# Rotary's swapped halves in one VectorE step, and the product with 1/rms of queries and keys on POOL, in a two-layer encoder trunk

## The chip, the cores and the metric

The kernel runs on one core of one Trainium2 chip. The core has TensorE (PE in the profile, with its weight loads as PEld), VectorE (DVE), ScalarE (ACT), GpSimd (POOL) and a queue of SyncE (SP) that issues most DMAs. The metric is the time of one execution on the device in microseconds (us), lower is better; a kernel's time is the median of its runs. Before the change it is 1128.28 us, the median of three runs from 1127.73 to 1128.44.

## The reference

A trunk of two transformer layers over 512 tokens of width 1024, all in float32. Each layer has a token mixer with 12 query heads and 3 key/value heads of width 64, four more heads that attend to a memory of 256 tokens, an output projection, and a SwiGLU feed-forward of width 2816, each with RMS norms around it. Layer 0 (mixer A) attends in a band of 128 tokens to either side, with a sink logit per head, and rotates only the first 16 of 64 dimensions. Layer 1 (mixer B) attends globally, normalises every query and key head by its own RMS, and rotates all 64 dimensions by row and column of a grid:

```python
def apply_rotary(x, cos, sin):
    half = x.shape[-1] // 2
    x1, x2 = xf[..., :half], xf[..., half:]
    return jnp.concatenate([x1 * c - x2 * s, x2 * c + x1 * s], axis=-1)
...
def mixer_b(q, k, v, qk_g, cos_r, sin_r, cos_c, sin_c):
    q = axial_rope(rms_norm(q, qk_g[0]), cos_r, sin_r, cos_c, sin_c)
    k = axial_rope(rms_norm(k, qk_g[1]), cos_r, sin_r, cos_c, sin_c)
```

So a head x becomes x * cos plus its swapped halves times a signed sine, and in layer 1 the whole is multiplied by 1/rms(x). The factor 1/rms is one number per token and head, so it may be multiplied in before or after the rotation.

## The kernel before

**Numbers in two parts.** Float32 products are made of three TensorE products of a high and a low part (type fp32r). `split` (lines 252 to 262) makes them: ScalarE rounds the high part (L258), VectorE subtracts it to get the low part (L262). Flags in the table `PACE` send some of either to POOL (L256, L260). Weights, hidden rows, queries, keys, and probabilities all pass through such a split.

**The mixer.** Tokens are in four tiles of 128 rows (t = 0 to 3). Keys and values come first (`kv_pieces`), then queries in groups of four heads (`q_pieces`, c = 0 to 2, and c = 3 for the memory heads). One tile of a query group runs like this: TensorE multiplies the hidden rows with the weights, 24 matmuls of 256 columns (L248 to L250); ScalarE copies the result out as `qx` (L488 in layer 1, L490 in layer 0); `rope` rotates it in place; ScalarE and VectorE split it into `q2` (L258, L262); TensorE transposes it (L502), and ScalarE copies the transpose into `qT` (L503). Keys do the same in 192 columns as `kx`, with a copy of the high part on POOL (L380) and transposes at L387 and L392.

**Rotary.** `rope_a` (layer 0, L400 to L403) works on 16 of 64 elements of each head: two VectorE products write the swapped halves times the sine into `rt`, one multiplies `x` with the cosine in place, one adds. `rope_b` (layer 1) has on ScalarE the squares (L411), on VectorE their sum per head (L412), on POOL 1/rms in two steps, a multiply-add and a power (`rstd`, L276 and L277, tile `r`), and on VectorE the two products of the halves (L419), the product with the cosine (L420), the sum (L421) and the product with 1/rms (L422). There are 16 such tiles in each layer: four of keys, twelve of queries. L258 of `q` or `k` waits for L422.

**Attention.** `score` makes a head's scores for one tile of queries (L526, L527), VectorE takes the row minimum of the negated scores (L537; with mask and sink in layer 0, L532), ScalarE the exponential with its sum (L538). After the fourth tile `normalise` inverts the sums on VectorE (L574, tile `rd`) and POOL scales the four tiles `p` (L577). `turn` transposes `p` on TensorE (L587) into one of two PSUM buffers `tp`, which a split empties into `th` (ScalarE) and `tl` (VectorE); `value` multiplies them with V (L601, L602), and ScalarE and VectorE add the two halves of the result into `tok` (L609, L610).

**What sets the order.** TensorE's order is written out by hand: `mixer` puts every piece into a list with a due time, taken from `PACE`, and issues the pieces in the order of these times. Queries of group c + 1 are made while the heads of group c attend. On the other engines a planner orders the instructions when the kernel is built: it simulates the engines with costs of its own and lets each take, of what is ready, the instruction that stands first in the program. In the trace VectorE's steps of one rotation are thus mixed with row minima and splits. On the chip each engine then runs its list strictly in order and waits on semaphores.

Of the kernel before, what the change touches and what calls it, by code (L numbers as in the profile page):

```python
# [13 lines left out]
OP = mybir.AluOpType  # L14
AX = mybir.AxisListType

P = 128
# [8 lines left out]
HD = 64  # L26
# [153 lines left out]
class Trunk:  # L180
# [212 lines left out]
        nc.vector.tensor_copy(kb[:, :, c], tp[:, :n])  # L393


    def rope_a(self, x, t, n):
        v = self.nc.vector
        tmp = self.core.tile([P, 4, 16], F32, tag="rt", name="rt", bufs=2)
        cs, sn = self.ropet[:, 0, t], self.ropet[:, 1, t]
        v.tensor_mul(tmp[:, :n, 0:8], x[:, :n, 8:16], sn[:, None, 0:8].to_broadcast([P, n, 8]))  # L400
        v.tensor_mul(tmp[:, :n, 8:16], x[:, :n, 0:8], sn[:, None, 8:16].to_broadcast([P, n, 8]))
        v.tensor_mul(x[:, :n, 0:16], x[:, :n, 0:16], cs[:, None, :].to_broadcast([P, n, 16]))
        v.tensor_add(x[:, :n, 0:16], x[:, :n, 0:16], tmp[:, :n])  # L403

    def rope_b(self, x, t, n, z):

        nc = self.nc
        v = nc.vector
        sq = self.core.tile([P, 4, HD], F32, tag="rt", name="sq", bufs=2)
        ss = self.small.tile([P, 4], F32, tag="ss4", name="ss4", bufs=2)  # L410
        nc.scalar.activation(sq[:, :n], x[:, :n], AF.Square)  # L411
        v.tensor_reduce(ss[:, :n], sq[:, :n], axis=AX.X, op=OP.add)  # L412
        r = self.small.tile([P, 4], F32, tag="r4", name="r4", bufs=3)
        self.rstd(r[:, :n], ss[:, :n], HD)
        tmp = self.core.tile([P, 4, HD], F32, tag="rt", name="rt", bufs=2)
        gc, gs = self.gt[:, z, 0, t], self.gt[:, z, 1, t]
        for h in range(2):
            o, i = slice(32 * h, 32 * h + 32), slice(32 - 32 * h, 64 - 32 * h)
            v.tensor_mul(tmp[:, :n, o], x[:, :n, i], gs[:, None, o].to_broadcast([P, n, 32]))  # L419
        v.tensor_mul(x[:, :n], x[:, :n], gc[:, None, :].to_broadcast([P, n, HD]))  # L420
        v.tensor_add(x[:, :n], x[:, :n], tmp[:, :n])  # L421
        v.tensor_mul(x[:, :n], x[:, :n], r[:, :n, None].to_broadcast([P, n, HD]))  # L422

    def rope(self, l, x, t, n, z):
        (self.rope_b(x, t, n, z) if l else self.rope_a(x, t, n))
# [794 lines left out]
```

## Time and profile before

| | |
|---|---|
| median of three runs | 1128.28 us (1127.73 to 1128.44) |
| profiled execution, its own time | 1127.18 us |
| its span, first to last instruction | 1125.4 us |
| granted TensorE clock | 0.999 |
| share of the span that engines are busy | PE 98%, PEld 89%, VectorE 75%, ScalarE 59%, POOL 19% |

The slices of 1/40 of the span (28 us each) show where each engine is busy, in tenths:

```profile
PE   9999999999999999999999999999999999999997
DVE  5788885999448757875888998757996378669854
ACT  6678984765435624563567888756664255345631
POOL 5693331102000000000445643312000000000001
```

The attention of layer 0 lies in the first six slices, that of layer 1 in slices 20 to 26; there POOL is in use, while the two feed-forwards use it hardly at all. A row of a timeline has the start (us from the first instruction), the time taken, engine, line, operation, what it writes and reads, how many instructions were merged, and in brackets the idle time before it with what ended it. Rows of waits give the waiting instruction, the one that ended the wait, the sum in us, how many, and the longest.

### The profile page before, as it was taken

The page shows a single profiled execution, that of the slowest core. Times are in us where ns is not written, and L with a number is a line of the kernel's source. Part 1 is how long each engine was busy: PE and PEld are TensorE (multiplying, and loading weights), DVE is VectorE, ACT ScalarE, POOL GpSimd, SP SyncE. Part 2 cuts the span into 40 slices and gives each one's busy share as a digit, 9 for nine tenths or more (in the row PEclk, how much of TensorE's full clock was granted, in tenths as well). Part 3 has the DMA queues.
Part 4 walks back from the last instruction along what each step waited for, and adds up shares of the span by engine and source line. Part 5 has one row for each costly group of instructions (what it writes and reads, how often), then busy time and mean ns, then how long its engine had stood idle before and what let it go on. Part 6 is the DMA issues. An engine that isn't in the chain of part 4 may idle for free.

```text
span 1125.4 us, 19486 instructions
## 1 busy us (share of the span) xinstructions
PE 1098.2 (98%) x7463; PEld 1004.6 (89%) x7463; DVE 841.8 (75%) x1431; ACT 658.8 (59%) x1347; POOL 214.6 (19%) x356
## 2 busy tenths in 40 slices
PE   9999999999999999999999999999999999999997
PEld 7899988899889989998897888878999899899985
DVE  5788885999448757875888998757996378669854
ACT  6678984765435624563567888756664255345631
POOL 5693331102000000000445643312000000000001
PEclk9999999999999999999999999999999999999999
DMA  6521016443413322325542100145135123413243
GB/s 236 197 85 39 20 57 220 155 132 124 151 38 113 132 94 76 113 90 192 187 150 76 39 20 18 40 149 188 38 113 168 58 75 113 150 61 99 88 166 112
DMA packets 34220, 123.02 MB, mean 109 GB/s; under 512 B 3920, under 2 KB 4304, under 8 KB 34000
## 3 DMA queue, kind: packets, MB, share of 16 engines
q1 hardware_dynamic: 33984, 121.66, 32.5%
q8 instruction: 58, 0.95, 0.3%
q14 instruction: 34, 0.28, 0.1%
q10 hardware_dynamic: 144, 0.14, 0.0%
HBM read 111.29 MB, written 10.49 MB: 108 GB/s over the span
## 4 chain that ended last, share of the span: by engine, by line
PE 66%; DVE 7%; ACT 4%; POOL 2%; issue 2%; POOLq 0%; DVEq 0%; ACTq 0%
PE ps L954 12%; PE ps L955 12%; PE ps L956 12%; PE ps L249 9%; PE ps L248 9%; PE ps L250 9%; PE tp L587 1%; DVE wlo L262 1%; POOL r L277 1%; PE o L602 1%; ACT whi L258 1%; DVE nm L537 1%; PE o L601 1%; DVE tl L262 1%; ACT p L538 1%
## 5 line engine op out<-in xcount | busy, mean ns | idle before, releaser
L258 ACT ACTIVATE whi<-raw 128x512 fp32r<-128x512 f32 (+2 forms) x190 | 157.1, 840 | 184.5 <-PE ps L956 94.7
L262 DVE TENSOR_TENSOR wlo<-raw,whi 128x512 fp32r<-128x512 f32 (+2 forms) x178 | 171.7, 974 | 69.9 <-ACT whi L258 69.1
L954 PE MATMUL ps<-sf,whi 128*128 128x256 f32 x640 | 179.9, 281 | 0.2
L955 PE MATMUL ps<-sf,wlo 128*128 128x256 f32 x640 | 179.8, 281 | 0.0
L956 PE MATMUL ps<-sf,whi 128*128 128x256 f32 x640 | 179.7, 281 | 0.0
L248 PE MATMUL ps<-whi,f 128*128 128x512 f32 x352 | 137.2, 390 | 0.0
L249 PE MATMUL ps<-wlo,f 128*128 128x512 f32 x352 | 137.1, 389 | 0.0
L250 PE MATMUL ps<-whi,f 128*128 128x512 f32 x352 | 137.0, 389 | 0.0
L956 PE MATMUL ps<-a,whi 128*128 128x256 f32 x480 | 134.4, 280 | 0.0
L954 PE MATMUL ps<-a,whi 128*128 128x256 f32 x480 | 134.3, 280 | 0.0
L955 PE MATMUL ps<-a,wlo 128*128 128x256 f32 x480 | 133.8, 279 | 0.0
L954 PEld LDWEIGHTS ps<-sf,whi 128*128 128x128 f32 x640 | 121.1, 189 | 1.1 <-ACT p L960 0.6
L955 PEld LDWEIGHTS ps<-sf,wlo 128*128 128x128 f32 x640 | 121.4, 190 | 0.5
L956 PEld LDWEIGHTS ps<-sf,whi 128*128 128x128 f32 x640 | 121.4, 190 | 0.0
L286 POOL TENSOR_SCALAR e<-sso 128x1 f32<-128x1 f32 x8 | 3.4, 422 | 566.1 <-ACT junk L281 566.0
L248 PE MATMUL ps<-whi,hT 128*128 128x256 f32 (+1 forms) x320 | 98.8, 309 | 0.0
L577 POOL TENSOR_SCALAR p<-p,rd 128x256 f32<-128x256 f32 (+2 forms) x128 | 79.1, 637 | 99.2 <-DVE rd L574 53.1
L249 PE MATMUL ps<-wlo,hT 128*128 128x256 f32 (+1 forms) x320 | 94.0, 294 | 2.1 <-DVE wlo L262 1.9
L250 PE MATMUL ps<-whi,hT 128*128 128x256 f32 (+1 forms) x320 | 93.7, 293 | 0.0
L955 PEld LDWEIGHTS ps<-a,wlo 128*128 128x128 f32 x480 | 90.5, 188 | 0.2
L954 PEld LDWEIGHTS ps<-a,whi 128*128 128x128 f32 x480 | 90.4, 188 | 0.2
L956 PEld LDWEIGHTS ps<-a,whi 128*128 128x128 f32 x480 | 90.1, 188 | 0.0
(201 smaller groups left out, 2750.7 us busy)
## 6 DMA issues: line engine op xcount, KB each, us to landing
raw<-in_wgu_dram SPq DMA_DIRECT2D x48, 512.0 KB, 4.4
raw<-in_wd_dram SPq DMA_DIRECT2D x44, 512.0 KB, 4.2
rb<-in_wgu_dram SPq DMA_DIRECT2D x40, 512.0 KB, 3.6
raw<-in_wq_dram SPq DMA_DIRECT2D x16, 512.0 KB, 4.5
raw<-in_wo_dram SPq DMA_DIRECT2D x16, 512.0 KB, 3.6
xt<-x SPq DMA_DIRECT2D x12, 512.0 KB, 4.6
raw<-in_wm_dram SPq DMA_DIRECT2D x8, 512.0 KB, 4.1
x<-y SPq DMA_DIRECT2D x8, 512.0 KB, 2.9
```

The lines of the kernel that those rows point to most:

```text
L248: mm(out, lh, rh, start=first, stop=False)
L249: mm(out, lh, rl, start=False, stop=False)
L250: mm(out, ll, rh, start=False, stop=last)
L258: nc.scalar.activation(hi, src, AF.Copy)
L262: nc.vector.tensor_sub(lo, src, hi.bitcast(F32))
L277: g.tensor_tensor(r, r, self.mhalf[:, :r.shape[1]], op=OP.pow)
L537: nc.vector.tensor_reduce(nm[:, i:i + 1], s[:, :n], axis=AX.X, op=OP.min)
L538: nc.scalar.activation(p[:, :n], src[:, :n], AF.Exp, bias=nm[:, i:i + 1], scale=-1.0, accum_out=den[:, i:i + 1])
L577: self.pooled = nc.gpsimd.tensor_scalar(hd["p"][z][:, :n], hd["p"][z][:, :n], rd[:, z:z + 1], 1.0, op0=OP.mult, op1=OP.mult)
L954: mm(out, wh[:, s], rh, start=start and k == 0, stop=False, skip_group_check=True)
L955: mm(out, wl[:, s], rh, start=False, stop=False, skip_group_check=True)
L956: mm(out, wh[:, s], rl, start=False, stop=k == 3, skip_group_check=True)
```

## The change

Both rotations now write the swapped halves in one VectorE step. `halves` views the last dimension as two halves; the input is read with the order of the halves reversed, a negative stride of one half, 8 elements in layer 0 and 32 in layer 1. That is one VectorE instruction less per tile, in all 32 tiles. In layer 1 the last product, with 1/rms, goes to POOL, which makes 1/rms in the two steps before it: 16 instructions leave VectorE's queue and enter POOL's, and the split of the tile on ScalarE and VectorE now waits for POOL.

```diff
+    def halves(self, x):
+        return x.rearrange("p n (h d) -> p n h d", h=2)
+
     def rope_a(self, x, t, n):
...
-        v.tensor_mul(tmp[:, :n, 0:8], x[:, :n, 8:16], sn[:, None, 0:8].to_broadcast([P, n, 8]))
-        v.tensor_mul(tmp[:, :n, 8:16], x[:, :n, 0:8], sn[:, None, 8:16].to_broadcast([P, n, 8]))
+        v.tensor_mul(self.halves(tmp[:, :n]), self.halves(x[:, :n, 0:16])[:, :, ::-1],
+                     self.halves(sn[:, None, :].to_broadcast([P, n, 16])))
...
     def rope_b(self, x, t, n, z):
...
-        for h in range(2):
-            o, i = slice(32 * h, 32 * h + 32), slice(32 - 32 * h, 64 - 32 * h)
-            v.tensor_mul(tmp[:, :n, o], x[:, :n, i], gs[:, None, o].to_broadcast([P, n, 32]))
+        v.tensor_mul(self.halves(tmp[:, :n]), self.halves(x[:, :n])[:, :, ::-1],
+                     self.halves(gs[:, None, :].to_broadcast([P, n, HD])))
         v.tensor_mul(x[:, :n], x[:, :n], gc[:, None, :].to_broadcast([P, n, HD]))
         v.tensor_add(x[:, :n], x[:, :n], tmp[:, :n])
-        v.tensor_mul(x[:, :n], x[:, :n], r[:, :n, None].to_broadcast([P, n, HD]))
+        nc.gpsimd.tensor_tensor(x[:, :n], x[:, :n], r[:, :n, None].to_broadcast([P, n, HD]), op=OP.mult)
```

## The prediction

> **What bounds the kernel now.** I read the page first, then the stretches that hold the rotary steps, then the waits of TensorE in those stretches.
>
> ```profile
> span 1125.4 us, 19486 instructions
> PE 1098.2 (98%) x7463; PEld 1004.6 (89%) x7463; DVE 841.8 (75%) x1431; ACT 658.8 (59%) x1347; POOL 214.6 (19%) x356
> ```
>
> TensorE is busy for 98% of the span. All idle time of TensorE together is 1125.4 - 1098.2 = 27.2 us, and no change to VectorE or POOL can win more than its part of that. The change touches two stretches: the mixer of layer 0 (here 15 to 116 us) and that of layer 1 (here its queries, from 584 us). The columns of the next view are the stretch, its length, and the busy time of PE, PEld, DVE, ACT and POOL.
>
> ```profile
> 15.00:116.00 101.00, 97.43 (x726) 92.04 (x725) 81.64 (x227) 76.23 (x205) 64.55 (x106) 1.00 0.31 108
> 584.00:605.00 21.00, 19.30 (x139) 17.39 (x138) 16.67 (x42) 12.43 (x30) 9.19 (x14) 1.00 0.32 100
> 605.00:672.00 67.00, 62.70 (x436) 54.80 (x435) 63.24 (x128) 56.52 (x133) 40.56 (x50) 1.00 0.08 25
> ```
>
> The last row matters most. There VectorE is busy for 63.24 of 67 us, more than TensorE, so two engines share the bound; POOL has 26 us free. What TensorE waits for, from 584 to 672 us:
>
> ```profile
> PE tp L587 <- DVE tl L262: 2.2, 3, 1.0
> PE ps L249 <- DVE wlo L262: 1.1, 1, 1.1
> PE o L601 <- DVE tok L610: 0.9, 1, 0.9
> PE tp L587 <- POOL p L577: 0.9, 2, 0.5
> PE tp L502 <- DVE q L262: 0.5, 1, 0.5
> ```
>
> and from 15 to 120 us:
>
> ```profile
> PE tp L315 <- DVE mT L262: 1.4, 1, 1.4
> PE tp L587 <- POOL p L577: 1.1, 2, 0.8
> PE tp L587 <- DVE tl L262: 0.3, 1, 0.3
> PE tp L587 <- DVE qx L402: 0.2, 1, 0.2
> ```
>
> So 5.6 us of waits in layer 1, of which 4.7 us end with VectorE, and in layer 0 some 1.9 us that end with it. These few microseconds are what can be won, and a wait on POOL already stands among them.
>
> **The change part by part.** The durations are minimum / median / maximum in ns.
>
> ```profile
> L400 DVE TENSOR_TENSOR rt<-qx,cst x12: 159/193/525, 42.5 to 110.1; 128x32 f32<-128x32 f32 x12
> L401 DVE TENSOR_TENSOR rt<-qx,cst x12: 183/186/1348, 42.6 to 110.1; 128x32 f32<-128x32 f32 x12
> L402 DVE TENSOR_TENSOR qx<-qx,cst x12: 214/226/580, 42.8 to 110.8; 128x64 f32<-128x64 f32 x12
> L419 DVE TENSOR_TENSOR rt<-qx,gt x24: 275/284/1385, 584.6 to 664.6; 128x128 f32<-128x128 f32 x24
> L420 DVE TENSOR_TENSOR qx<-qx,gt x12: 408/418/909, 585.3 to 665.5; 128x256 f32<-128x256 f32 x12
> L422 DVE TENSOR_TENSOR qx<-qx,r x12: 407/426/861, 587.1 to 667.4; 128x256 f32<-128x256 f32 x12
> L621 POOL TENSOR_TENSOR gt<-ru x2: 737/1228/1720, 274.2 to 274.9; 128x256 f32<-128x256 f32 x2
> ```
>
> One step for the two halves. Two operations of layer 1 (2 x 284 ns) become one over 256 elements, which L420 prices at 418: 150 ns less per tile, 2.4 us over 16 tiles if the narrower key tiles save as much. In layer 0 it is 193 + 186 - 226 = 153 ns, again about 2.4 us. No row shows a negative stride. Inside a half the elements still lie side by side, so I take the plain price; the bounds are that (0.41 us) and every element at half speed (2 x 418 = 0.84 us). [...]
>
> The product with 1/rms. L422 leaves VectorE: 12 x 0.426 us, and for the four key tiles at three quarters of the width as an estimate 4 x 0.32, together 6.4 us. POOL gets 16 products of two inputs. L621 is the same kind and size on POOL: 0.74 us for the first, 1.72 for the second. I take 0.74, the undisturbed one, and keep 1.72 as the upper bound. For 16 that is up to 11.8 us, and POOL has the room. VectorE sheds 2.4 + 6.4 = 8.8 us in layer 1. What that is worth depends on the place.
>
> First group of queries. A wait is removed here, and a chain made longer.
>
> ```profile
> 588.02 0.43 DVE L262 TENSOR_TENSOR q<-qx,q 128x256 fp32r<-128x256 f32 x1 [0.48 <-ACT q L258]
> 588.50 0.53 PE L502 MATMUL tp<-identr,q 128*128 128x128 f32 x4
> 592.42 0.51 PE L502 MATMUL tp<-identr,q 128*128 128x128 f32 x4 [0.48 <-DVE q L262]
> 593.94 0.43 DVE L421 TENSOR_TENSOR qx<-qx,rt 128x256 f32<-128x256 f32 x1
> 595.26 0.43 DVE L422 TENSOR_TENSOR qx<-qx,r 128x256 f32<-128x256 f32 x1 [0.90 <-POOL r L277]
> 595.61 1.28 DVE L262 TENSOR_TENSOR wlo<-raw,whi 128x512 fp32r<-128x512 f32 x2
> 596.34 0.39 PE L249 MATMUL ps<-wlo,hT 128*128 128x256 f32 x1 [1.13 <-DVE wlo L262]
> ```
>
> The transposes of the first two tiles start 0.05 us after, or wait for, the split that ends the rotary chain. A product of 0.74 in place of 0.43 puts 0.31 us on each: +0.62 us (0, if ScalarE evicts the next tile ahead of the waiting split, to 2 x 1.29 = 2.6 with the long product). Behind the waiting split stand on ScalarE the eviction of the next tile and the key copies. The third tile pays in the other direction: VectorE stood 0.90 us waiting for r, with the weight split that TensorE needed behind it. Without L422 that split follows L421 at 594.37 instead of 595.61, 1.24 us earlier, and the wait of 1.13 us goes: -1.13 us (0 to -1.13). Next late is nothing that the view shows.
>
> The first head's probabilities.
>
> ```profile
> 612.88 1.01 POOL L277 TENSOR_TENSOR r<-r,mhalf 128x4 f32<-128x4 f32 x1
> 613.88 3.24 POOL L577 TENSOR_SCALAR p<-p,rd 128x512 f32<-128x512 f32 x4
> 614.46 0.41 DVE L421 TENSOR_TENSOR qx<-qx,rt 128x256 f32<-128x256 f32 x1
> 615.39 0.41 DVE L422 TENSOR_TENSOR qx<-qx,r 128x256 f32<-128x256 f32 x1
> 617.18 0.33 PE L587 MATMUL tp<-cst,p 128*128 128x128 f32 x1 [0.44 <-POOL p L577]
> ```
>
> TensorE takes each of these p as POOL finishes it. The product becomes ready at 614.87, in the middle of the four, and stands earlier in the program, so I put it between them: +0.74 us (0 behind them; if POOL waits for it ahead of them, 614.87 - 613.88 + 0.74 = +1.7). For the next head the view has:
>
> ```profile
> 619.93 3.13 POOL L577 TENSOR_SCALAR p<-p,rd 128x512 f32<-128x512 f32 x4 [0.82 <-DVE rd L574]
> 625.21 0.60 PE L587 MATMUL tp<-cst,p 128*128 128x128 f32 x4
> ```
>
> Its four p end at 623.06 and its transposes start at 625.21, which covers one product; I take the same for the heads behind it.
>
> The crowded stretch. Four waits, 2.2 us for tl and 0.9 for tok, end with VectorE.
>
> ```profile
> 629.25 0.43 DVE L422 TENSOR_TENSOR qx<-qx,r 128x256 f32<-128x256 f32 x1 [0.31 <-POOL r L277]
> 629.60 0.68 DVE L262 TENSOR_TENSOR tl<-tp,th 128x512 fp32r<-128x512 f32 x1
> 637.56 2.87 POOL L577 TENSOR_SCALAR p<-p,rd 128x512 f32<-128x512 f32 x4
> 637.66 0.86 DVE L422 TENSOR_TENSOR qx<-qx,r 128x256 f32<-128x256 f32 x1
> ```
>
> Ahead of each stands an L422 that goes: with its wait 0.74 us in the first, 0.86 us in the second, about 0.41 in the calmest, and the merged step gives 0.15 more each. That covers the three tl waits and over half of the tok wait: 2.2 + 0.5 = 2.7. L422 took 0.86 instead of 0.41 with POOL scaling p beside it; POOL's own products will stretch other two-input steps in the same way, so I give one such lengthening back: 2.7 - 0.4, -2.3 us (0 to -3.1).
>
> Layer 0. The wait for mT and the two short ones stand behind keys' and queries' rotary steps: 0.15 us each, -0.45 us (0 to -1.9).
>
> **Sum:** 0.62 - 1.13 + 0.74 - 2.3 - 0.45 = -2.5 us. The profiled execution took 1127.18 us around its span of 1125.4, 1.10 us under the median of 1128.28; the sum gives 1124.7 for it, and on the scale of the median 1125.8 us.
>
> **The rivals.**
>
> [...] A two-input product on POOL and two-input steps on VectorE lengthen each other: L421's kind of step takes 0.41 to 0.86 us, L621 0.74 to 1.72. If each of 16 products costs VectorE the 0.43 us that L422's worst row shows, 6.9 of the 8.8 us return, the crowded stretch wins 0.5 instead of 2.3, by the fifth of the relief that is left, and the rest (-0.2) remains: 1128.28 - 0.7 = 1127.6. For it speaks that POOL is busy 40.56 of 67 us there; against it that the steps reading PSUM (tl, row maxima) run at their usual length beside it. A stride that halves the rate ends in the same place: 16 x (0.84 - 0.57) = 4.3 us come back. [...]
>
> The queue makes it slower. POOL runs in order. If the products stand behind the four p, the one at 614.87 starts at 617.12 and ends at 617.86, 2.1 us later than L422 ended (615.80). ScalarE keeps its order, so its split of q holds the exponentials and probability copies behind it for 2.1 us, in each of the seven tiles from 612 us on that meet four p (three of the second group of queries, four of the third). ScalarE has 67 - 56.52 = 10.5 us free there, 1.5 per tile; 0.6 x 7 = 4.2 us reach TensorE, the gain of the stretch is lost, and the rest (-0.51 and -0.45) stays: 1128.28 + 3.2 = 1131.5. It decides from a hold of 1.5 us. Against it: r, issued just before the product, ran ahead of the p at 612.88.
>
> All waits on VectorE go. No cost at the first group and at the p: -(1.1 + 2.2 + 0.9 + 0.5) - 1.9 = -6.6, 1121.7 us. Against it: TensorE that comes sooner meets the next late tile.
>
> **How the numbers follow.** A measurement of this kernel tells about 0.2%, 2.3 us, from no change. The forecast gets 0.50, the port 0.25, the queue 0.17, all waits gone 0.08. The forecast's own range, 1123.5 to 1127.5, is set by the place of the product (+0.74 from 0 to 1.7) and by the crowded stretch; its middle lies 0.2 us beyond the mark, and I give 0.33 of its 0.50 to faster. Faster: 0.33 + 0.08 = 0.41. Slower: the queue, 0.17, and 0.02 for long products at the first group. The same: 0.40. The range reaches to 1122.7, short of all waits gone, and up to 1130.6, where the queue costs three quarters of its price.
>
> **What would show it.** In the changed kernel's groups L422's successor on POOL at 0.74 to 0.9 us and the merged step at 0.42 (0.23 in layer 0). The wait for wlo at 596 us gone. The wait of the first head's transposes for p longer by 0.7. The waits for tl between 625 and 672 us under 1 us in sum, and VectorE 5 us or more less busy from 605 to 672. The forecast is wrong if ScalarE's waits for the POOL product exceed 1.5 us per tile, or if VectorE stays above 61 us busy in those 67.

## The result, and the profile after

The change makes the kernel slower. Its median is 1133.6 us (four runs, 1133.17 to 1134.24) against 1128.05 us before (four runs, 1127.73 to 1128.44): a ratio of 1.0052 as recorded (the two medians alone give 1.0049), 95% interval 1.0038 to 1.0065. The forecast was 1125.8 us, and 1130.6 us was the top of the range.

The head of the changed kernel's page; its execution took 1133.17 us:

```profile
span 1131.4 us, 19447 instructions
...
PE 1099.2 (97%) x7463; PEld 1004.6 (89%) x7463; DVE 831.1 (73%) x1383; ACT 657.2 (58%) x1347; POOL 224.5 (20%) x372
```

VectorE has lost 10.7 us of work and POOL has gained 9.9, as the change says. TensorE is busy for 1099.2 instead of 1098.2 us and idle for 32.2 instead of 27.2: of the 6.0 us by which the span grew, 5.0 are waiting. In the stretches of layer 1 (columns as in the prediction; the second is 5 us longer now):

```profile
584.00:605.00 21.00, 19.56 (x144) 17.94 (x143) 13.94 (x31) 11.24 (x26) 9.30 (x15) 1.00 0.28 90
605.00:677.00 72.00, 63.09 (x430) 54.17 (x429) 58.63 (x116) 56.97 (x136) 46.06 (x62) 1.00 0.10 30
```

The relieved VectorE is busy for 58.63 of 72 us, now less than TensorE (63.09); before it was busier than TensorE (63.24 against 62.70 of 67). Yet TensorE waits more. Before, ScalarE and VectorE waited from 584 to 680 us for, among others:

```profile
ACT q L258 <- DVE qx L422: 7.7, 5, 2.2
...
DVE q L262 <- ACT q L258: 1.0, 2, 0.5
...
DVE tl L262 <- ACT th L258: 0.3, 1, 0.3
```

The waits of ScalarE, VectorE and TensorE in the changed kernel in the same window (lines from L400 on have moved by two to three: the product is L424 on POOL, the exponential L540, the transposes of `p` L589; the split stays L258 and L262):

```profile
ACT q L258 <- POOL qx L424: 19.5, 11, 2.6
...
DVE q L262 <- ACT q L258: 12.4, 11, 2.4
DVE tl L262 <- ACT th L258: 3.5, 9, 0.7
...
PE tp L589 <- DVE tl L262: 6.2, 5, 1.6
PE s L528 <- ACT p L540: 1.5, 2, 0.9
PE tp L504 <- DVE q L262: 1.4, 2, 0.7
PE tp L589 <- POOL p L579: 0.7, 2, 0.3
```

This is a chain over four engines. ScalarE's split of `q` waits 19.5 us for the product, which POOL now makes, instead of 7.7. VectorE's low part of `q` waits for the split, 12.4 us instead of 1.0. Behind both stand `th` and `tl`, and TensorE's wait for `tl` has grown from 2.2 to 6.2 us. The waits for `wlo` (1.1) and `tok` (0.9) are gone.

One tile shows the link. Before, on ScalarE and POOL (its four `p` at 637.56 and its L422 at 637.66 stand in the prediction):

```profile
636.40 1.17 POOL L277 TENSOR_TENSOR r<-r,mhalf 128x4 f32<-128x4 f32 x1
...
637.33 0.59 ACT L609 ACTIVATE tmp<-o 64x512 f32<-64x512 f32 x1 [0.47 <-PE o L602]
637.95 0.60 ACT L258 ACTIVATE th<-tp 128x512 fp32r<-128x512 f32 x1
638.56 0.42 ACT L258 ACTIVATE q<-qx 128x256 fp32r<-128x256 f32 x1
```

The same tile in the changed kernel, POOL first, then ScalarE, then VectorE:

```profile
641.78 1.20 POOL L277 TENSOR_TENSOR r<-r,mhalf 128x4 f32<-128x4 f32 x1
642.99 0.70 POOL L579 TENSOR_SCALAR p<-p,rd 128x512 f32<-128x512 f32 x1
643.65 0.61 POOL L424 TENSOR_TENSOR qx<-qx,r 128x256 f32<-128x256 f32 x1
...
642.49 0.59 ACT L611 ACTIVATE tmp<-o 64x512 f32<-64x512 f32 x1 [0.53 <-PE o L604]
644.30 0.42 ACT L258 ACTIVATE q<-qx 128x256 fp32r<-128x256 f32 x1 [1.22 <-POOL qx L424]
644.62 0.58 ACT L258 ACTIVATE th<-tp 128x512 fp32r<-128x512 f32 x1
...
644.75 0.46 DVE L262 TENSOR_TENSOR q<-qx,q 128x256 fp32r<-128x256 f32 x1 [0.72 <-ACT q L258]
645.24 0.69 DVE L262 TENSOR_TENSOR tl<-tp,th 128x512 fp32r<-128x512 f32 x1
```

Two things are new. The split of `q` now stands ahead of `th` in ScalarE's list; before it stood behind. And the product is late: POOL puts one scaling of `p` between the power and the product, so that the product ends 1.27 us after the power (643.65 + 0.61 - 642.99) and not 0.95 (638.52 - 637.57). In all four tiles where a scaling stands between (here called the loop tiles) it ends 1.27 us after; before, it was 0.46 us in the first of them and 0.95 in the others. Before, `th` started right behind `tmp`; now it starts 1.54 us after the end of `tmp` (644.62 - 643.08). The matmuls that consume all this slip as follows, the same matmul in the two timelines, starts in us:

| waits for | before | after | later by |
|---|---|---|---|
| `q`, first group | 588.50 | 589.84 | 1.34 |
| `wlo` before, nothing after | 596.34 | 596.64 | 0.30 |
| an exponential | 608.34 | 610.38 | 2.04 |
| `tl` | 620.55 | 624.79 | 4.24 |
| `tl` | 632.06 | 637.20 | 5.14 |
| `tl` | 659.86 | 666.32 | 6.46 |
| `tl` | 669.73 | 675.70 | 5.97 |

In this execution TensorE is 0.64 us behind already at 584.09 us, ahead of all these rows (584.73). Two runs with the same layer 0 (e15_late_dve and e16_later below) lie at -0.44 and 0.65 us there, so this is spread of single executions and no part of the loss.

The loss arises between 597 and 660 us, and most of it ahead of the waits on which the prediction had put its gain: TensorE is 4.24 us behind at 620.55, and what follows adds 1.7 net (5.97 at 669.73). The first jump, by 1.8 us between 605 and 608 us, comes from the first group of queries. Its fourth split and ScalarE's first exponential, before and after:

```profile
601.02 0.42 ACT L258 ACTIVATE q<-qx 128x256 fp32r<-128x256 f32 x1 [1.22 <-DVE qx L422]
...
607.33 0.69 ACT L538 ACTIVATE p<-s,nm 128x512 f32<-128x512 f32 x1
```

```profile
603.45 0.42 ACT L258 ACTIVATE q<-qx 128x256 fp32r<-128x256 f32 x1 [2.52 <-POOL qx L424]
...
609.54 0.69 ACT L540 ACTIVATE p<-s,nm 128x512 f32<-128x512 f32 x1
```

In that group the copy `qx` of a tile stands behind the split of a tile before it on ScalarE, so that the holds add up. TensorE's score matmuls then wait 0.3 us for `vm`, whose copy stands behind the fourth split on ScalarE, at 606.68, and 0.9 us for the late exponential at 610.38. Behind 675 us the kernel keeps the distance.

### The profile page after: what moved, and what is told of

It reads as the page before. It is cut to its first block, busy times and chain, and to the rows that moved or that the text cites. A ratio compares the mean times of both kernels' runs of the same rounds, so it can differ in the third digit from the quotient of the medians.

```text
span 1131.4 us, 19447 instructions
## 1 busy us (share of the span) xinstructions
PE 1099.2 (97%) x7463; PEld 1004.6 (89%) x7463; DVE 831.1 (73%) x1383; ACT 657.2 (58%) x1347; POOL 224.5 (20%) x372
## 4 chain that ended last, share of the span: by engine, by line
PE 66%; ACT 5%; DVE 4%; POOL 3%; issue 2%; POOLq 0%; DVEq 0%; ACTq 0%
PE ps L956 12%; PE ps L958 12%; PE ps L957 12%; PE ps L249 9%; PE ps L248 9%; PE ps L250 9%; PE tp L589 1%; POOL r L277 1%; ACT p L540 1%; ACT whi L258 1%; PE o L604 1%; DVE wlo L262 1%; ACT th L258 1%; PE o L603 1%; DVE tl L262 1%
## 5 line engine op out<-in xcount | busy, mean ns | idle before, releaser
L258 ACT ACTIVATE whi<-raw 128x512 fp32r<-128x512 f32 (+2 forms) x190 | 157.3, 840 | 184.4 <-PE ps L958 94.7
L262 DVE TENSOR_TENSOR wlo<-raw,whi 128x512 fp32r<-128x512 f32 (+2 forms) x178 | 171.5, 972 | 70.1 <-ACT whi L258 69.2
```

The lines of the kernel that those rows point to most:

```text
L258: nc.scalar.activation(hi, src, AF.Copy)
L262: nc.vector.tensor_sub(lo, src, hi.bitcast(F32))
```

## The experiments

All were timed in the same way, beside runs of the kernel before on the same chip; the medians of those were 1127.13 to 1127.47 us, so that ratios compare better than times. Where an expectation gives its theories letters, they hold for the runs of one question.

### Which part of the change costs the time

e1_merge has the merged halves in both layers and the product on VectorE; e3_merge0 merges in layer 0 alone, e4_merge1 in layer 1 alone. e2_pool moves only the product:

```diff
-        v.tensor_mul(x[:, :n], x[:, :n], r[:, :n, None].to_broadcast([P, n, HD]))
+        nc.gpsimd.tensor_tensor(x[:, :n], x[:, :n], r[:, :n, None].to_broadcast([P, n, HD]), op=OP.mult)
```

> Merged halves in both layers, product with 1/rms left on VectorE. Hold theory (the loss comes from ScalarE's split of q, which now stands in ScalarE's list ahead of exponentials and th copies and waits 19.5 us in 11 tiles for POOL's product): the splits wait for VectorE again, some 8 us in sum, TensorE's waits for tl return to about 2 us, and the time is 1127.0 to 1129.0. Merge theory (the shorter rotation makes the planner put the rest in another, worse order, or the negative stride costs): half or more of the loss is here, 1131 or above.

> Product with 1/rms on POOL alone, the two halves as before. Hold theory: most of the 5.6 us of loss, 1132 to 1134, with ScalarE's splits of q waiting 15 us or more for POOL. Merge theory: 1127 to 1130.

> Merged halves in layer 0 alone. In the changed kernel TensorE runs 0.5 to 0.7 us behind the kernel before from 113 us on and keeps that through the feed-forward: if the merged step of layer 0 makes it, 1128.6 to 1128.9; if it is chance of one profile, 1128.0 as before; by my forecast's term 1127.6.

> Merged halves in layer 1 alone. Hold theory: 1127 to 1128.5, since VectorE sheds 2.4 us in its crowded stretch and nothing waits for POOL that did not before. Merge theory: 1130 or above.

| kernel | median us | ratio to before | 95% interval |
|---|---|---|---|
| e1_merge | 1127.71 | 1.0003 | 0.9994 to 1.0011 |
| e2_pool | 1133.04 | 1.005 | 1.0037 to 1.0063 |
| e3_merge0 | 1127.63 | 1.0001 | 0.9992 to 1.001 |
| e4_merge1 | 1127.83 | 1.0002 | 0.9994 to 1.0011 |

The move of the product is the whole loss. The merged step is worth nothing that can be measured, in neither layer, though the step itself takes what it should. Three groups of the changed kernel, minimum / median / maximum in ns:

```profile
L403 DVE TENSOR_TENSOR rt<-qx,cst x12: 194/224/597, 42.5 to 110.0; 128x64 f32<-128x64 f32 x12
...
L420 DVE TENSOR_TENSOR rt<-qx,gt x12: 412/416/741, 585.8 to 670.2; 128x256 f32<-128x256 f32 x12
...
L424 POOL TENSOR_TENSOR qx<-qx,r x12: 612/614/734, 588.3 to 672.5; 128x256 f32<-128x256 f32 x12
```

The step with the negative stride takes 416 ns, like the product with the cosine (418 in the prediction's rows), so the lower bound of the prediction held. The product on POOL takes 614 ns and at most 734. The rival that two-input steps on both engines lengthen each other falls, as the cause of the loss, with these rows and with VectorE's busy time: of the 11.2 us that the prediction's prices give for both layers (8.8 and 2.4), 10.7 came off. Of the 36 steps that VectorE has left in the rotation of the query tiles of layer 1 (products and sum), five took 0.49 to 1.19 us and the others 0.41 to 0.43; the five ran beside POOL's weight splits (L260) or its scaling of `p`, none beside the product.

### Is it the late 1/rms?

e5_r_cheap keeps the change but leaves out the power: a multiplication stands in its place. e6_column leaves 63 of the 64 columns of each head's product on VectorE and gives POOL the last one, so that the split still waits for POOL:

```diff
-        self.rstd(r[:, :n], ss[:, :n], HD)
+        nc.gpsimd.tensor_scalar(r[:, :n], ss[:, :n], 1.0 / HD, EPS, op0=OP.mult, op1=OP.add)
+        nc.gpsimd.tensor_scalar(r[:, :n], r[:, :n], 0.5, 1.0, op0=OP.mult, op1=OP.mult)
```

```diff
-        nc.gpsimd.tensor_tensor(x[:, :n], x[:, :n], r[:, :n, None].to_broadcast([P, n, HD]), op=OP.mult)
+        v.tensor_mul(x[:, :n, :63], x[:, :n, :63], r[:, :n, None].to_broadcast([P, n, 63]))
+        nc.gpsimd.tensor_tensor(x[:, :n, 63:], x[:, :n, 63:], r[:, :n, None], op=OP.mult)
```

> The changed kernel with the power of 1/rms left out: POOL's second step for r is a multiplication, so q and k are scaled by half their mean square instead of 1/rms, and the output is not the reference's. The power took 1.0 to 1.2 us of POOL, a multiplication of four columns some 0.2. Nothing else of the work, and hardly the order, changes. Hold theory: every split of q on ScalarE waits about 1 us less for POOL's product (from 19.5 us in sum to under 11), and more than half of the loss goes: 1127.5 to 1130.5. [...]

> The changed kernel with 63 of 64 columns of the product back on VectorE and only the last column on POOL. The wait of ScalarE's split for a POOL step stays, POOL's work of 9.4 us nearly goes, and the planner puts ScalarE's splits in the same places as in the kernel with the merged halves alone. Hold theory (what costs is the early place of the split in ScalarE's list, with the product late): 1127.3 to 1129. If any wait on POOL behind VectorE costs by itself: 1130 or above. [...]

e5_r_cheap: 1125.15 us, ratio 0.9982 (0.9974 to 0.9991). Its lists on ScalarE and VectorE are those of the changed kernel, instruction for instruction; only the product comes sooner. POOL's power step of e5_r_cheap, and its waits from 584 to 680 us:

```profile
635.03 0.38 POOL L418 TENSOR_SCALAR r<-r 128x4 f32<-128x4 f32 x1
...
ACT q L258 <- POOL qx L425: 11.4, 11, 2.0
...
DVE q L262 <- ACT q L258: 4.8, 6, 1.7
```

0.38 instead of 1.20 us for the power takes 8 us off ScalarE's and VectorE's waits each, and turns a loss of 0.52% into a gain of 0.18%. With these lists, then, the time hangs on when the product arrives.

e6_column: 1127.94 us, 1.0007 (0.9998 to 1.0015), no change. Here the split waits for POOL as well, 14.4 us in 11 waits, but the planner gave ScalarE the list of e1_merge. ScalarE's list from its first exponential of the stretch on, [Q] the split of `q`:

```
before      exp exp [Q] exp qx exp sq kma exp kma qT exp qx exp [Q] sq exp th th exp qT whi th whi [Q] exp th ... tmp exp [Q] th
e1, e6      exp [Q] exp exp qx exp sq kma exp kma qT exp qx exp [Q] sq exp th th qT exp whi [Q] th whi exp th ... tmp exp [Q] th
after, e5   exp [Q] exp exp qx exp sq kma exp kma qT exp [Q] qx exp sq exp th th exp [Q] qT whi th whi exp th ... tmp [Q] exp th
e7, e8      exp exp exp [Q] qx exp sq kma exp kma qT exp qx exp [Q] sq exp th th qT exp whi whi th exp th exp [Q] ...
```

With the product on POOL the planner puts several splits one exponential or one copy earlier. What differs between e6_column and the changed kernel is this list, VectorE's load, and a little of the lateness (the product ends 1.1 us after the power in the loop tiles instead of 1.27, and 0.5 instead of 0.7 in the first group); the wait for POOL is in both.

### Is it the place of the split?

e7_behind keeps the change and puts the splits of the groups c = 1 and 2 behind, to a due time 0.8 of a head later; e8_behind_dve is the same with the product on VectorE; its splits stand at the same places among the exponentials, though from 648 us on some copies around them are swapped.

```diff
+                def later():
+                    with self.tc.issue_after(self.last):
+                        halve()
+                if l and c in (1, 2):
+                    put(x0 + (t + 0.75) * PACE[l]["qstep"] + BEHIND, later)
+                else:
+                    halve()
```

> The changed kernel, the products on POOL as they are, but the split of q of the second and third group of queries is issued 0.8 of a head later, behind a later exponential on ScalarE. Hold theory: the waits of these eight splits for POOL go, those of the first group stay (some 9.5 us of 19.5), nothing else of the work changes, and the loss between 605 and 677 us goes: 1126.5 to 1129. [...]

> The same later split, with the product on VectorE: merged halves and the order of ScalarE's list the same as in the run before this one. The pair gives the worth of the move to POOL with no split held by it. [...] Its own time: 1127 to 1129.

e7_behind: 1125.88 us, 0.9987 (0.9978 to 0.9996), faster than before. e8_behind_dve: 1126.8 us, 0.9995 (0.9986 to 1.0004). So a later place takes the loss away. I took the place for the cause, and tested it from the other side: e11_order has the product on VectorE and the changed kernel's places, made by ordering edges such as

```diff
+        with self.behind("exp", self.count("exp", sink is None)):
             nc.scalar.activation(p[:, :n], src[:, :n], AF.Exp, bias=nm[:, i:i + 1], scale=-1.0,
                                  accum_out=den[:, i:i + 1])
```

which queue the next exponential, copy or transpose's copy behind the split. All eight splits stand ahead of the same exponential as in the changed kernel; five stand exactly there, three one or two copies later (the second behind `qx`, the third behind two `whi`, the eighth behind `th` and `whi`). e9_half, e12_bit, e10_late and e16_later are e7_behind with 0.55, 0.45, 1.0 and 1.2 of a head.

> The product stays on VectorE (merged halves as in e1_merge), but ScalarE's list is given the order that the planner made with the product on POOL: of the eight splits of q in the groups c = 1 and 2, five stand one exponential or one probability copy earlier than in e1_merge. Theory A (the loss lies in the place of the split in ScalarE's list; 1/rms is late in both kernels because its power takes 1.0 to 1.2 us on POOL, so the split holds ScalarE whoever makes the product): 1130.5 to 1133 us, and ScalarE's waits for the product between 584 and 680 us at 14 us or more instead of e1_merge's 10.0. Rival B (the place matters little; it is the product that comes later from POOL): 1127.2 to 1128.2 us, as e1_merge with 1127.7, and waits near 10 us.

> As e7_behind, with the split of q put 0.55 instead of 0.8 of a head behind its product. Its splits of the groups c = 1 and 2 stand at or behind their places in the kernel before in seven of eight tiles. Theory A (place in ScalarE's list): 1125.5 to 1127 us, near e7_behind's 1125.9. Rival B (it is the late product, whatever the place): nearer to the changed kernel, 1129 us or more.

> As e7_behind with 0.45 of a head. The first three splits of q of the groups c = 1 and 2 keep the early places of the changed kernel, the other five stand one place further back. Theory A: between the changed kernel and e7_behind, by the share of the tiles that keep their early place 1126.5 to 1130 us. Rival B: 1131 us or more.

> As e7_behind with a whole head (1.0). The split stands behind two more exponentials or copies; ScalarE's waits for the product nearly vanish (under 6 us between 584 and 680), but the transposes of q follow the split sooner. Theory A: 1124.8 to 1126.5 us if the transposes of q still find their tile, up to 1129 us if TensorE waits for q there.

> As e10_late with 1.2 of a head. ScalarE's waits for the product shrink a little more; the split of q comes 1 to 2 us later and the transposes of q, which already waited 2.2 us in three places in e10_late, wait longer. Where these decide: 1125 to 1127 us; where they don't: 1123.5 to 1124.5 us.

| split later by (heads) | kernel | median us | ratio to before | 95% interval |
|---|---|---|---|---|
| 0 | changed kernel | 1133.6 | 1.0052 | 1.0038 to 1.0065 |
| 0.45 | e12_bit | 1128.47 | 1.0011 | 1.0003 to 1.002 |
| 0.55 | e9_half | 1127.64 | 1.0005 | 0.9997 to 1.0014 |
| 0.8 | e7_behind | 1125.88 | 0.9987 | 0.9978 to 0.9996 |
| 1.0 | e10_late | 1124.46 | 0.9975 | 0.9966 to 0.9985 |
| 1.2 | e16_later | 1134.46 | 1.0061 | 1.0047 to 1.0075 |
| 0, product on VectorE | e11_order | 1128.25 | 1.001 | 1.0001 to 1.0019 |

The series goes the way of theory A up to 1.0, with e9_half 0.6 us above its range and e10_late 0.3 us below it; e10_late is faster than both kernels, though ScalarE still waits 9.5 us for the product there and not under 6. These 9.5 us are the four splits of the first group, which no run of this series moved; the eight splits that were moved wait no more. At 1.2 the split is too late: e16_later was expected at 1127 us at most, and the last section shows what it lost. And e11_order is a miss: 1130.5 to 1133 us were expected. The early place by itself costs about 0.07% over e1_merge, which is within the two intervals (e1_merge has the first split early too). Waits of e11_order (split L272 and L276, product L439):

```profile
ACT q L272 <- DVE qx L439: 12.3, 10, 2.8
...
DVE qx L439 <- POOL r L292: 4.4, 9, 0.9
...
DVE q L276 <- ACT q L272: 1.2, 3, 0.5
...
PE tp L607 <- DVE tl L276: 2.2, 4, 0.7
```

ScalarE is held ten times here too, but for less, and VectorE hardly: its low part of `q` waits 1.2 us instead of 12.4. Theory A fell in its simple form. Neither the late product alone (e6_column) nor the early place alone (e11_order) costs what the two cost together.

### Late product and early place together

e18_p_place takes the lateness out and leaves the lists: in four tiles POOL makes the product directly behind the power, and the first `p` comes behind it. The lists of ScalarE and VectorE in the stretch are the changed kernel's. e17_p_behind has the same on POOL, but lets the planner place the splits again; they then move one copy further forward, ahead of `tmp`.

```diff
+            with self.tc.issue_after(self.scaled) if self.ahead else contextlib.nullcontext():
                 self.pooled = nc.gpsimd.tensor_scalar(hd["p"][z][:, :n], hd["p"][z][:, :n], rd[:, z:z + 1], 1.0,
                                                       op0=OP.mult, op1=OP.mult)
```

> The changed kernel with one difference: in the four loop tiles (c, t) = (1, 3), (2, 0), (2, 1), (2, 2) POOL makes the product directly behind its power, and the scaling of the first p that stood between them (0.69 to 0.70 us) comes behind it. The lists of ScalarE and of VectorE in the stretch are instruction for instruction those of the changed kernel. Theory C (lateness of the product in an early place): 0.65 us less hold in each of four tiles, 1129 to 1131.5 us, with ScalarE's waits for the product from 584 to 680 us at 16 to 17.5 instead of 19.5 us. Rival D (that scaling is the whole loss): 1127 to 1129 us. Rival E (the lists alone decide, whenever the product comes): 1133 us and more, by up to 0.6 us per head that now gets its first p later.

> As e18_p_place, but the planner is left to place the split of q anew: it stands one copy earlier, ahead of tmp, and VectorE's sum into tok behind the low part of q. Theory C: the hold that e18_p_place took away comes back in part on tmp and tok, 1129.5 to 1132.5 us, slower than e18_p_place by 0.3 to 1.5 us. Rival D: within 0.5 us of e18_p_place.

e18_p_place: 1130.74 us, 1.0032 (1.0019 to 1.0044), as theory C had it. e17_p_behind: 1133.27 us, 1.0054 (1.004 to 1.0067), in C's direction and 0.8 us above its range (2.5 us over e18_p_place, where 0.3 to 1.5 were expected). Waits of e18_p_place (product L429):

```profile
ACT q L262 <- POOL qx L429: 17.0, 11, 2.7
...
DVE q L266 <- ACT q L262: 9.8, 9, 2.4
...
PE tp L599 <- DVE tl L266: 4.3, 5, 1.3
```

0.6 us less lateness in each of four tiles (the product ends 0.69 instead of 1.27 us after the power) takes 2.5 us from ScalarE's waits (19.5 to 17.0), 2.6 from VectorE's and 1.9 from TensorE's wait for `tl`, and 0.20% from the time. One place forward (e17_p_behind) gives it back. With e5_r_cheap, which also leaves both lists alone, this shows the cause: the product is late against the place that the planner gave to the split that waits for it, and the split holds ScalarE and VectorE with `th`, the exponentials and `tl` behind it.

e13_next and e14_next_place were to test the same before that:

```diff
+        if first:
+            for ins in self.scales:
+                self.tc.add_manual_dep(ins, scaled.name, mybir.DependencyInfo(
+                    mybir.DependencyClass.NoSync, mybir.DependencyReason.DATA), reason="order")
```

> The changed kernel, with the product put directly behind its power on POOL in the four loop tiles (c, t) = (1, 3), (2, 0), (2, 1), (2, 2), where one scaling of p (0.69 to 0.70 us) stood between; the four p of that head come behind. The planner then moves the split of q a further step forward in ScalarE's list. Theory C (what counts is by how much the product is later than the place of the split allows): the product comes 0.65 us sooner but the split stands one probability copy earlier as well, so most of the hold stays: 1130.5 to 1133 us. Rival D (the scaling of p between power and product is the whole loss): 1127.5 to 1129.5 us.

> As e13_next, but the four splits of q are kept at the places they have in the changed kernel, behind the copy tmp. Only the 0.65 us of lateness in four tiles is taken away. Theory C: 0.65 us less hold on ScalarE and VectorE in each of four tiles, of which 0.4 to 1.0 us per tile reached TensorE: 1129 to 1131.5 us, and ScalarE's waits for the product from 584 to 680 us at 16 to 17.5 instead of 19.5 us. Rival D: 1127 to 1129 us. If the lateness plays no part (the place alone), 1133 us; e11_order, with this place and the product on VectorE, was 1128.25.

They took 1161.53 us (1.0304, 1.029 to 1.0318) and 1161.67 us (1.0305, 1.029 to 1.0319), and answer another question. The edit caught the four `p` of the head before, which until then ran long ahead of the product, and put them behind it. TensorE's wait in e13_next from 584 to 700 us, and one stretch of it:

```profile
PE tp L595 <- POOL p L584: 21.5, 18, 4.8
...
630.00:660.00 30.00, 20.17 (x96) 16.52 (x97) 13.43 (x25) 12.31 (x27) 12.09 (x16) 0.77 0.10 33
```

18 transposes wait 21.5 us for `p`: so much does an order on POOL weigh where it is really wrong.

### What the move is worth where it does no harm

e15_late_dve is e10_late with the product back on VectorE, splits at the same places among the exponentials.

> e10_late (split a whole head behind, 1124.46 us) with the product on VectorE again and the same places of the splits among the exponentials and copies. If the move to POOL relieves VectorE as the prediction's step on the crowded stretch said (0.41 us and more ahead of each tl), this is 1125.5 to 1127 us, 1 to 2.5 us slower than e10_late. If the late split is the whole gain, it is 1124.3 to 1125 us.

e15_late_dve: 1123.75 us, 0.9971 (0.996 to 0.9983), the fastest kernel of the study; e10_late, with the product on POOL, has 0.9975 (0.9966 to 0.9985). At 0.8 of a head the order is the other way round (e8_behind_dve 0.9995, e7_behind 0.9987), with intervals that overlap as well. So the move is worth nothing that can be told, and the gain of e10_late is the later split. TensorE's waits in e15_late_dve from 584 to 680 us, where three waits for `tl` took 2.2 us before:

```profile
PE ps L250 <- DVE wlo L263: 1.1, 1, 1.1
...
PE tp L600 <- DVE tl L263: 0.2, 1, 0.2
```

The product still stands on VectorE, and the waits for `tl` are gone all the same. Its place has changed: before, L422 at 629.25 stood ahead of the `tl` at 629.60; here the same `tl` starts at 626.91 and the product behind it, at 627.49.

## Why the prediction was wrong

**The bound and the prices** were read rightly. The few microseconds of idle time and their holders were where the money was, in both directions. The merged step costs 0.416 us (0.418 taken), the product on POOL 0.61 us (0.74 taken, so 0.13 too dear).

**First group.** Forecast +0.62 and -1.13 at three matmuls. The same matmuls give +0.62 and +0.24 for the two waits for `q`, and -1.28 for the wait for `wlo`, which is gone as foretold: near, with the first wait at twice its price of 0.31. But the step ended there, with "Next late is nothing that the view shows". The splits hold ScalarE through all four tiles, and TensorE pays 1.8 us for it at 608 us, a term that the sum doesn't have.

**First head's `p`.** Forecast +0.74 for a product between the four `p`. In the changed kernel's timeline POOL puts it behind them:

```profile
617.02 2.87 POOL L579 TENSOR_SCALAR p<-p,rd 128x512 f32<-128x512 f32 x4
619.86 0.61 POOL L424 TENSOR_TENSOR qx<-qx,r 128x256 f32<-128x256 f32 x1
...
620.50 0.42 ACT L258 ACTIVATE q<-qx 128x256 fp32r<-128x256 f32 x1 [2.21 <-POOL qx L424]
```

The wait for `p` is 0.7 instead of 0.9 us, the bound "0 behind them". But the split stands still for 2.21 us, so the price is paid there: TensorE falls back by 1.5 us, from 2.76 at 617.18 to 4.24 at 620.55.

**Layer 0 and the merged step.** Forecast -0.45 us, and 0.15 per tile in the crowded stretch. e3_merge0 shows no change. e4_merge1 shows none either, but by its trace a gain and a loss cancel: TensorE loses 1.6 us from 608.34 to 620.55, where the first split now stands an exponential earlier, and wins 1.5 us from there to 669.73.

**The crowded stretch** is the term that went most astray: forecast -2.3 us, measured +1.7 from 620.55 to 669.73. It failed twice. It took L422 for a cost that goes only when L422 leaves VectorE; in e15_late_dve it stays, only behind `tl` instead of ahead of it, and the waits go. And it let the product go while everything else kept its place. The product's end moved from 0.46 or 0.95 to 1.27 us after the power in the loop tiles, the split of `q` moved forward at the same time, and ScalarE and VectorE were held, with `th` and `tl` behind them. The 0.4 us that the term gives back, for steps of VectorE stretched by POOL's products, are not shown there: the sums into `tok` that ran beside a product took 0.67 to 0.70 us (0.68 in the mean before). One step of VectorE was longer beside a product, a weight split of 1.07 us at 583.53, ahead of the stretch; before the change the split at 583.66 took 0.74.

**The step that failed** is thus the same in all three places: the sum priced the moved product at the instruction that waits for it and put at nothing what stands behind that instruction on ScalarE. That wait grew from 7.7 to 19.5 us. The reason for the early places lies in the planner, whose costs are its own: it places the split as if 1/rms and product came sooner than a power of 1.0 to 1.2 us allows; e5_r_cheap, with a power step of 0.38 us, makes the planned lists good. That the planner's cost for the power is what errs is inferred from this; its costs themselves weren't read.

**The rivals.** The queue named the right holder, ScalarE's split with the exponentials and copies behind it, the sign, and 3.2 of the 5.6 us. Its cause (a product behind four `p`) holds in one tile only, the one at 617 us, and it counted on "ScalarE keeps its order". Its test came true: the forecast was to be wrong if ScalarE's waits for the product exceed 1.5 us per tile, and they are 19.5 / 11 = 1.8. The rival with the chance of 0.25 (in the chances "the port": two-input steps on POOL and VectorE that lengthen each other) is refuted as the cause, and no run shows a port that the two share; its evidence was thin too, since beside the 0.86 us row stand the prediction's own rows at 614.46 and 615.39, where two-input steps took 0.41 us beside the same kind of four `p`. The case in which all waits on VectorE go needs the later split: e15_late_dve reaches -3.4 us of it. One slip of the chances: the middle of the forecast's own range, 1125.5, lies 0.5 us and not 0.2 beyond the mark of 2.3 us.

**How the loss divides**, by the ratios: merged step 0.03%, early place 0.07% (e11_order over e1_merge), the scaling of `p` between power and product 0.20% (the changed kernel over e18_p_place), and 0.22% (2.5 us) between e11_order and e18_p_place: the product on POOL itself. Each difference has an uncertainty of about 0.15%, so only the last two stand out.

The traces show where. The table has how many us later than before the same matmul starts, less what the run was behind at 584.09 us; the head names the matmul by its start before:

| kernel | 604.91 | 608.34 | 617.18 | 620.55 | 669.73 |
|---|---|---|---|---|---|
| e1_merge | 0.0 | 0.0 | 1.2 | 1.6 | 0.1 |
| e11_order | -0.1 | -0.1 | 1.1 | 1.1 | 0.3 |
| e18_p_place | -0.4 | 1.4 | 2.1 | 3.6 | 3.3 |
| changed kernel | -0.4 | 1.4 | 2.1 | 3.6 | 5.3 |
| e10_late | -0.5 | 1.4 | 0.7 | 0.6 | -2.8 |

What e18_p_place loses to e11_order it has lost by 620.55 us, in two jumps: at 608 us, from the first group, and at 620 us, from the tile in which the product stands behind four `p`. What the changed kernel loses beyond that comes behind 620.55, in the loop tiles. The jump at 608 us is there in e10_late too, and in every other run with the whole product on POOL behind a power (1.6 to 1.9 us), and in none with it on VectorE; with later splits it is won back. How each part splits between ScalarE's list and VectorE's stays open: both engines were held in every kernel that lost by the move.

## What to carry to other kernels

A step moved to another engine is not priced by its duration and the load of the two engines, but by when its result arrives against the place of the next instruction that waits for it: read off what stands behind that instruction on its engine, and on the engine that waits for that one. If a planner with its own costs orders the lists, look whether it moves the waiting instruction too; here it moved it forward while the input came later. A wait that keeps turning up beside the bound may be cheaper to remove by issuing the consumer later (here 0.29% for a split one head later) than by relieving the engine, up to the point where the next consumer starts to wait.

## What the runs showed of the hardware that was not expected

The power of 128x4 numbers on POOL takes 1.0 to 1.2 us in the twelve query tiles of the changed kernel, nearly twice the product of 128x256 numbers (0.61 us) and three times a multiplication of the same four columns (0.38 us in e5_r_cheap's row at 635.03).

The granted clock fell to 0.57 over 4 us of e16_later, behind a wait of 2.41 us. In that kernel the transposes of `q` come too early for the late split; their wait from 584 to 700 us and four stretches (the third number from the end is the granted clock):

```profile
PE tp L515 <- DVE q L263: 8.5, 6, 2.4
...
612.00:616.00 4.00, 1.59 (x16) 1.32 (x14) 3.55 (x9) 3.58 (x11) 2.29 (x4) 1.00 0.16 64
616.00:620.00 4.00, 4.00 (x19) 3.81 (x20) 1.24 (x2) 0.90 (x2) 2.42 (x4) 0.57 0.00 0
...
624.00:628.00 4.00, 2.32 (x13) 2.05 (x14) 2.13 (x6) 2.46 (x7) 3.92 (x6) 0.80 0.02 4
628.00:632.00 4.00, 4.00 (x23) 3.62 (x22) 1.82 (x3) 2.39 (x6) 2.60 (x3) 0.77 0.13 19
```

The wait of 2.41 us ended at 616.00. Behind it matmuls of 256 columns started 0.21 us apart (616.81 to 617.66), ahead of it 0.12 us apart (611.86 to 612.22). Behind another wait, of 2.02 us, that ended at 625.68, they started 0.21 us apart again (626.49 to 626.92), and the granted clock was 0.80 from 624 to 628 us and 0.77 from 628 to 632; in e13_next, with waits up to 4.8 us, it was 0.77 over 30 us. In the changed kernel, whose longest wait in the stretch is 1.6 us, the clock stayed at 1.00. So a split that is 0.2 of a head too late (e16_later over e10_late) costs 10.0 us, of which 6.3 are longer waits for `q` (8.5 against 2.2); the clock that was not granted in the three stretches of 4 us (0.43, 0.20 and 0.23) is at most another 3.4, as an estimate.
